# First loads on two queues, products of ones ahead of the first weights, and squares summed by additions

## The chip, the cores and the metric

The kernel runs on one core of a Trainium2 chip. The metric is the device time of one execution in microseconds (us); lower is better. Times below are of single executions, and the median of several is compared.

## The reference

Two transformer blocks run one after the other on one sequence of 256 tokens with 2048 channels. The first ("hybrid") block normalises its input, multiplies by a wide weight matrix, and joins a forgetting attention with a recurrent (RWKV-like) branch. The second normalises again and joins a gated convolution, a latent attention and an attention over 256 memory tokens. What matters here is the root mean square norm, which stands at the head of each block, before the memory attention and inside the latent attention:

```python
def rms_norm(x, g):
    xf = x.astype(jnp.float32)
    y = xf * lax.rsqrt(jnp.mean(xf * xf, axis=-1, keepdims=True) + EPS)
    return (y * g.astype(jnp.float32)).astype(x.dtype)

h = _rmsnorm(x, norm_gain)
u = h @ w_in
```

All arithmetic is float32. The output is 256 x 2048.

## The kernel before

**Data and tiles.** Activations lie channel-major: a tile of kind `a4` holds 4 x 128 channels (128 partitions, 4 slices) of 256 tokens, so four such tiles hold an activation of 2048 channels. Weights come from memory in 658 blocks of 128 x 1024 floats (`raw`). `conv_to` (L399) splits every block into a high part, copied by ScalarE (`whi`, L407), and a rest, subtracted by VectorE (`wlo`, L408). A product with float32 precision is then three products in the faster float32r format (high x high, high x low, low x high). `mm` (L284) records every product, so all of them carry the line L287; `tt` (L240) records two-operand VectorE work at L242, `red` (L268) records reductions at L270, `act` (L272) all ScalarE work at L279.

**The beginning.** `par`, the table of gains, is loaded at L325 by SyncE's queue. `dma_to` (L380) loads in this order, all on the same queue: two halves of the first input tile `xt[0]` (L388), each followed by a half of the first weight block (L389), then whole blocks and the other three input tiles (L392, L396). The kernel does not wait for the norm before it multiplies: `start_tile` (L666) scales a tile by the gain and splits it into `xgh` and `xgl`, products with the groups `lora` and `r0` are accumulated over the four tiles (the loop at L716), and the results are scaled by the reciprocal root at the end. Beside this, `start_squares` (L680) squares each tile on ScalarE (`sq`, 128 x 1024) and sums the four channel slices on VectorE with one reduction over a transposed view (L683, `sqr`, 128 x 256). In the fourth round, four products with a matrix of ones (L724, `ssq`) add up over partitions and tiles, and `mean_rsqrt` (L645) turns the sum into the reciprocal root `rs`.

**The same sum elsewhere.** `sumsq_start` (L632), called by the memory job `mem_job` (L1279), has for each of four tiles a square, a reduction and a product with ones. `latent_job` (L1414), called for `cq` and `ckv`, has one square, one reduction (L1420) and one product with ones.

**The order of the work.** Large products are called group by group (`gemm`, L472). Smaller jobs are generators, spawned into a list; after each piece of a group `pump` (L459) steps them as far as a book of estimated engine times allows (`clock`, L232): each recorded operation adds an estimate to its engine's clock. The framework then arranges the recorded instructions of each engine by a simulated timeline; for example, the memset of L794 stands at 0.89 us and the load of L806 at 6.47 us, far ahead of their places in the code. On the chip every engine runs its list in that fixed order.

Of the kernel before, what the change touches and what calls it, by code (L numbers as in the profile page):

```python
# [14 lines left out]
ALU = mybir.AluOpType  # L15
# [212 lines left out]
def hybrid_kernel(ctx: ExitStack, tc: tile.TileContext, io, out):  # L228
    nc = tc.nc
    TE, ACT, DVE, POOL = nc.tensor, nc.scalar, nc.vector, nc.gpsimd  # L230
# [3 lines left out]
    def fsz(ap):  # L234
        n = 1
        for s in ap.shape[1:]:
            n *= s
        return n
# [5 lines left out]
    def mul(o, a, b):  # L244
        tt(o, a, b, ALU.mult)
# [22 lines left out]
    def red(o, a, op):  # L268
        clock["dve"] += CD + fsz(a) / 960.0
        DVE.tensor_reduce(out=o, in_=a, axis=AX.X, op=op)  # L270

    def act(o, a, f, scale=1.0, bias=None, accum=None):  # L272
        clock["act"] += CA + fsz(o) / 1200.0
        kw = {}
        if bias is not None:
            kw["bias"] = bias
        if accum is not None:
            kw["accum_out"] = accum
        ACT.activation(out=o, in_=a, func=f, scale=scale, **kw)  # L279
# [4 lines left out]
    def mm(o, l, r, start=True, stop=True):  # L284
        n = fsz(o)
        clock["pe"] += max(0.000424 * n, 0.0001 + 0.0016 * fsz(l) / 2) if l.dtype == F32R else max(0.00168 * n, 0.00168 * fsz(l))
        TE.matmul(o, lhsT=l, rhs=r, start=start, stop=stop)  # L287
# [13 lines left out]
    def nm(s):  # L301
        serial[0] += 1
        return f"{s}_{serial[0]}"

    def a4(name, dt=F32):
        return apool.tile([128, 4, 256], dt, name=nm(name), tag="a4")

    def b1(name, dt=F32, shape=(128, 256)):
        return spool.tile(list(shape), dt, name=nm(name), tag="b1")
# [7 lines left out]
    def bank(name):  # L317
        return ppool.tile([128, 512], F32, name=nm(name), tag="s")


    par = cpool.tile([128, NPAR], F32, name="par")
    con = cpool.tile([128, NCON2], F32, name="con")
    con1 = cpool.tile([128, NCON - NCON2], F32, name="con1", tag="early_late2")
    xt = [a4("xt") for _ in range(4)]
    nc.sync.dma_start(out=par, in_=io["params"])  # L325

    def pc(n, i=0, k=1, p0=0, p1=128):
        o = PCOL[n][0]
# [12 lines left out]
    one1 = cpool.tile([128, 1], F32, name="one1")  # L341
    DVE.memset(one1, 1.0)
    ones = one1.to_broadcast([128, 128])

    omm = cpool.tile([128, 34], F32, name="omm")
    hw0 = cpool.tile([128, 8], F32, name="hw0")
# [6 lines left out]
    def derive_params():  # L353
        mu0 = PCOL["mu_r"][0]
        ts(omm, par[:, mu0:mu0 + 34], -1.0, ALU.mult, 1.0, ALU.add)
        ts(hw0, pc("w0", 0, 8), 0.5, ALU.mult)
        ts(ha0, pc("a0", 0, 8), 0.5, ALU.mult)
        ts(ka2, pc("k_a", 0, 8), 0.5, ALU.mult)
        ts(oka, pc("k_a", 0, 8), -0.5, ALU.mult, 1.0, ALU.add)
        ts(qns, par[:, PCOL["qn_g"][0]:PCOL["qn_g"][0] + 2], 192.0 ** -0.5, ALU.mult)  # L360
        ts(mqs, pc("mqn_g", 0, 2), 256.0 ** -0.5, ALU.mult)
# [9 lines left out]
    def block_at(i):  # L371

        if i >= 12:
            return i
        return 4 + 2 * (i // 3) + i % 3 - 1 if i % 3 else i // 3

    def half(p):
        return slice(512 * p, 512 * p + 512)

    def dma_to(n):  # L380
        while st["dma"] < min(n, nblk):
            i = st["dma"]
            j = block_at(i)
            raw_t[j] = wpool.tile([128, 1024], F32, name=nm("raw"), tag="raw", bufs=NRAW)
            x = i // 3
            if i == 0:
                for p in range(2):
                    nc.sync.dma_start(out=xt[0][:, 2 * p:2 * p + 2, :], in_=io["xT"][:, 2 * p:2 * p + 2, :])  # L388
                    nc.sync.dma_start(out=raw_t[j][:, half(p)], in_=io["W"][j, :, half(p)])  # L389
            else:  # L390
                if i % 3 == 0 and x < 4:
                    nc.sync.dma_start(out=xt[x], in_=io["xT"][:, 4 * x:4 * x + 4, :])  # L392
                if i == 12:
                    nc.sync.dma_start(out=lw2f[0:96, :], in_=io["w2"])
                    nc.sync.dma_start(out=la2f[0:96, :], in_=io["a2"])
                nc.sync.dma_start(out=raw_t[j], in_=io["W"][j])  # L396
            st["dma"] += 1
# [155 lines left out]
    def new_pair(name):  # L553
        return a4(name + "h", F32R), a4(name + "l", F32R)
# [7 lines left out]
    def out4(name, dt=F32):  # L562
        return claim(a4(name, dt))
# [23 lines left out]
    def run(gen):  # L587
        for _ in gen:
            pass
# [39 lines left out]
    la2f = la2.rearrange("p a b -> p (a b)")  # L629
    dma_to(NRAW)  # L630

    def sumsq_start(tiles, scales=None):  # L632

        ps = bank("ssq")
        n = len(tiles)
        for i, x in enumerate(tiles):
            sq = a4("sq")
            act(sq, x, AF.Square)
            r = b1("sqr")
            red(r, sq.rearrange("p a t -> p t a"), ALU.add)  # L640
            yield
            mm(ps[:, :256], ones, r, start=i == 0, stop=i == n - 1)
        sumsq_start.out = ps[:, :256]

    def mean_rsqrt(ps, n, eps):  # L645
# [15 lines left out]
            yield  # L661

    xg = []
    r4 = a4("sqr")

    def start_tile(i):  # L666

        x = xt[i]
        p = new_pair("xg")
        xg.append(p)  # L670
        for cs in ((range(2), range(2, 4)) if i == 0 else (range(4),)):
            for c in cs:
                acopy(p[0][:, c, :], x[:, c, :], scale=pc("norm_gain", 4 * i + c))
            for c in cs:
                stt(p[1][:, c, :], x[:, c, :], pc("norm_gain", 4 * i + c), p[0].bitcast(F32)[:, c, :], ALU.mult,
                    ALU.subtract)
            if cs[0] == 0:
                conv_to(3 * i + 1)

    def start_squares(i):  # L680
        sq = a4("sq")
        act(sq, xt[i], AF.Square)
        red(r4[:, i, :], sq.rearrange("p a t -> p t a"), ALU.add)  # L683


    def shifted(dst, ps, key, c, p1=128):
# [23 lines left out]
            shifted(t[:, c, :], xs[:, c, :], key, 4 * b + c)  # L710
        return f

    ssq = bank("ssq")[:, :256]
    acc_l = [bank("lora")[:, :256] for _ in range(2)]
    acc_r = [gpool.tile([128, 512], F32, name=nm("acc.r0"), tag="g")[:, :256] for _ in range(4)]
    for b in range(4):  # L716
        start_tile(b)
        if b == 0:
            derive_params()
        conv_to(3 * b + 3)  # L720
        start_squares(b)
        if b == 3:
            for i in range(4):
                mm(ssq, ones, r4[:, i, :], start=i == 0, stop=i == 3)  # L724
            run(mean_rsqrt(ssq, 2048.0, 1e-6))
            rs = mean_rsqrt.out
            lr, evac = out4("lr"), evac_scaled("r", 0)
            conv_to(14)
        for acc, cols, blocks in ((acc_l, 256, [b]), (acc_r, 512, [4 + 2 * b, 5 + 2 * b])):
            per = 1024 // cols  # L730
            for c, o in enumerate(acc):
                for e, j in enumerate(blocks):
                    for i in range(per):
                        k = per * e + i
                        w = slice(i * cols + 128 * c, i * cols + 128 * c + 128)
                        xh, xl = xg[b][0][:, k, :], xg[b][1][:, k, :]
                        mm(o, hi_t[j][:, w], xh, start=b == 0 and k == 0, stop=False)
                        mm(o, hi_t[j][:, w], xl, start=False, stop=False)
                        mm(o, lo_t[j][:, w], xh, start=False, stop=b == 3 and k == 3)
                if b == 3:  # L740
                    if cols == 256:
                        key = ("wd", "ad")[c]
                        lora[key] = lr[:, 2 + c, :]
                        mul(lr[:, c, :], o, rs)
                        shifted(lora[key], lr[:, c, :], key, 0)
                    else:
                        evac(c, o)
            for j in blocks:
                del hi_t[j], lo_t[j]
    del ssq, r4  # L750

    def start_job():
        yield from norm_pairs(xt, lambda c: pc("norm_gain", c), rs, "h", h)
# [630 lines left out]
    def rope_tables():  # L1384
# [5 lines left out]
        ts(a, a, cc("invf"), ALU.mult)  # L1390
        ts(k, a, 1.0 / (2.0 * math.pi), ALU.mult, MAGIC, ALU.add)
        ts(k, k, -MAGIC, ALU.add)
        yield
# [20 lines left out]
    def latent_job(d, gain, name):  # L1414
        t = d[0]
        ps = bank("lss")
        sq = a4("lsq")
        act(sq, t, AF.Square)
        r = b1("lr")
        red(r, sq.rearrange("p a t -> p t a"), ALU.add)  # L1420
        yield
        mm(ps[:, :256], ones, r)
        yield
        ms = b1("lms")
        ts(ms, ps[:, :256], 1.0 / 512.0, ALU.mult, 1e-6, ALU.add)
        y, tmp, g = b1("ly"), b1("lt"), b1("lg")
        yield from rsqrt(ms, y, tmp, g)
        for c in range(4):
            stt(t[:, c, :], t[:, c, :], pc(gain, c), y, ALU.mult, ALU.mult)
        yield  # L1430
        p = new_pair(name)
        split(t, p[0], p[1])
        lat[name] = [p]
# [260 lines left out]
    for j in range(4):  # L1694
        p = out_pair("ol")
# [10 lines left out]
    for j in range(4):  # L1706
        gemm(f"gl{j}", h2, gate(gt))
        p = out_pair("mg")
# [17 lines left out]
        gemm(f"w2{j}", mg, evac_out(j))  # L1726


MAGIC = 12582912.0
TWO_PI = (6.28125, 0.0019350051879882812, 3.0199159819567e-07)  # L1730
NA4, NB1, NB2 = 33, 7, 5
# [39 lines left out]
```

## Time and profile before

| | before |
|---|---|
| median of 3 runs | 2058.69 us |
| lowest, highest run | 2053.68, 2060.20 us |
| the profiled execution's own time | 2059.04 us |
| its span from the first to the last instruction | 2057.2 us |
| PE busy | 2023.2 us (98%) |
| VectorE (DVE) busy | 1348.6 us (66%) |
| ScalarE (ACT) busy | 968.9 us (47%) |
| mean granted TensorE clock | 0.995 |

PE is TensorE's matrix product, PEld its weight load, SPq the queue that SyncE issues, "L287" line 287 of the kernel. A row of a timeline has the start, the duration of the group (both in us), engine, line, operation, the written tile and the read ones, their shapes, and in brackets how long the engine had been idle and what ended that. The chain of waits is the work that ended last, followed back from the last instruction.

### The profile page before, as it was taken

The numbers are of one execution on the slowest core, as the hardware profiler recorded it, in microseconds if no ns is written. First come the engines' busy times: TensorE is split into PE (matmuls) and PEld (weight loads), VectorE is DVE, ScalarE is ACT, GpSimd is POOL, SyncE is SP. The second block draws the span as 40 slices with busy tenths as digits, with TensorE's granted clock in tenths as the row PEclk, the third lists the DMA queues.
The fourth block names the chain that finished last, engine by engine and source line by source line (L and its number), as shares of the span: only waits on it lengthen the run. The fifth ranks groups of instructions, "written<-read, shape, count | busy, mean of one in ns | idle before, by whom it ended". The sixth has DMA issues, their size and how long they took to land.

```text
span 2057.2 us, 33333 instructions
## 1 busy us (share of the span) xinstructions
PE 2023.2 (98%) x13456; PEld 1820.6 (88%) x13456; DVE 1348.6 (66%) x1987; ACT 968.9 (47%) x1334; POOL 73.9 (4%) x133
## 2 busy tenths in 40 slices
PE   8999989999899999999999999999999999999999
PEld 8999889998677888898999899998788889988887
DVE  8776966879745578665865676755765655555554
ACT  6634435454344445554555445445545444444442
POOL 0002000010000000000000000000000000000000
PEclk9999999999999999999999999999999999999999
DMA  7555543645544756665655554556665655566664
GB/s 248 172 175 165 172 139 128 185 149 169 182 144 141 268 187 215 190 220 185 190 183 183 158 182 154 186 164 195 205 189 170 203 168 182 195 208 202 193 195 153
DMA packets 105674, 374.97 MB, mean 182 GB/s; under 512 B 12920, under 2 KB 13904, under 8 KB 105520
## 3 DMA queue, kind: packets, MB, share of 16 engines
q1 hardware_dynamic: 97568, 350.73, 53.1%
q0 software_dynamic: 7952, 22.12, 3.6%
q8 instruction: 105, 1.72, 0.4%
q14 instruction: 49, 0.40, 0.1%
HBM read 365.76 MB, written 5.86 MB: 181 GB/s over the span
## 4 chain that ended last, share of the span: by engine, by line
PE 89%; DVE 6%; issue 2%; DMA 2%; ACT 1%; POOL 0%; SPq 0%; DVEq 0%; ACTq 0%; POOLq 0%
PE acc.lz L287 4%; PE acc.gb L287 4%; PE acc.gl L287 4%; PE acc.gc L287 4%; PE acc.wo L287 4%; PE acc.w L287 4%; PE acc.lo L287 4%; PE acc.gm L287 4%; DVE wlo L242 2%; PE acc.fq L287 2%; PE acc.mz L287 2%; PE acc.mq L287 2%; PE acc.cz L287 2%; PE acc.cb L287 2%; PE acc.mk L287 2%; PE acc.zb L287 2%
## 5 line engine op out<-in xcount | busy, mean ns | idle before, releaser
L242 DVE TENSOR_TENSOR wlo<-raw,whi 128x1024 fp32r<-128x1024 f32 (+1 forms) x659 | 795.6, 1221 | 493.2 <-ACT whi L279 481.7
L279 ACT ACTIVATE whi<-raw 128x1024 fp32r<-128x1024 f32 (+1 forms) x659 | 683.3, 1055 | 758.6 <-issue 88.0
L287 PE MATMUL acc.lz<-h2h,whi 128*128 128x256 f32 x256 | 72.5, 283 | 0.0
L287 PE MATMUL acc.lz<-h2l,whi 128*128 128x256 f32 x256 | 72.5, 283 | 0.0
L287 PE MATMUL acc.lz<-h2h,wlo 128*128 128x256 f32 x256 | 72.4, 283 | 0.0
L287 PE MATMUL acc.ga<-wlo,hh 128*128 128x512 f32 x128 | 52.3, 410 | 1.9 <-DVE wlo L242 1.9
L287 PE MATMUL acc.gb<-whi,hh 128*128 128x512 f32 x128 | 50.1, 400 | 1.1 <-ACT gate L279 1.1
L287 PE MATMUL acc.ga<-whi,hl 128*128 128x512 f32 x128 | 51.1, 404 | 0.0
L287 PE MATMUL acc.gb<-wlo,hh 128*128 128x512 f32 x128 | 50.6, 399 | 0.0
L287 PE MATMUL acc.gb<-whi,hl 128*128 128x512 f32 x128 | 50.4, 398 | 0.0
L287 PE MATMUL acc.ga<-whi,hh 128*128 128x512 f32 x128 | 50.3, 403 | 0.0
L287 PE MATMUL acc.gl<-wlo,h2h 128*128 128x512 f32 x128 | 50.0, 392 | 0.0
L287 PE MATMUL acc.gl<-whi,h2h 128*128 128x512 f32 x128 | 50.0, 392 | 0.0
L242 DVE TENSOR_TENSOR W<-W,W 64x1 f32<-64x1 f32 (+30 forms) x62 | 48.7, 785 | 2.1
L287 PE MATMUL acc.gc<-whi,h2l 128*128 128x512 f32 x128 | 50.0, 392 | 0.0
L287 PE MATMUL acc.gl<-whi,h2l 128*128 128x512 f32 x128 | 50.0, 392 | 0.0
L287 PE MATMUL acc.w<-wlo,mgh 128*128 128x512 f32 x128 | 49.9, 390 | 0.0
L287 PE MATMUL acc.w<-whi,mgl 128*128 128x512 f32 x128 | 49.9, 390 | 0.0
L287 PE MATMUL acc.gm<-wlo,h2h 128*128 128x512 f32 x128 | 49.9, 391 | 0.0
L287 PE MATMUL acc.gc<-wlo,h2h 128*128 128x512 f32 x128 | 49.9, 391 | 0.0
L287 PE MATMUL acc.gm<-whi,h2l 128*128 128x512 f32 x128 | 49.8, 390 | 0.0
L287 PE MATMUL acc.wo<-whi,ml 128*128 128x512 f32 x128 | 49.5, 389 | 0.0
(627 smaller groups left out, 6223.9 us busy)
## 6 DMA issues: line engine op xcount, KB each, us to landing
raw<-in_W SPq DMA_DIRECT2D x657, 512.0 KB, 4.0
hr<-hd POOLq DMA_DIRECT2D x10, 512.0 KB, 5.2
hr<-hd POOLq DMA_DIRECT2D x12, 256.0 KB, 6.5
xr<-in_xtm POOLq DMA_DIRECT2D x4, 512.0 KB, 6.3
mt<-in_memT POOLq DMA_DIRECT2D x4, 512.0 KB, 6.2
xbd<-x1g POOLq DMA_DIRECT2D x4, 512.0 KB, 3.0
xo<-xbd POOLq DMA_DIRECT2D x4, 512.0 KB, 5.3
out_tm<-xo SPq DMA_DIRECT2D x8, 256.0 KB, 4.5
```

The costliest lines, as they stand in the source:

```text
L242: DVE.tensor_tensor(out=o, in0=a, in1=b, op=op)
L279: ACT.activation(out=o, in_=a, func=f, scale=scale, **kw)
L287: TE.matmul(o, lhsT=l, rhs=r, start=start, stop=stop)
```

## The change

Three things are changed.

1. The loads of `par` and of the two halves of `xt[0]` are issued by ScalarE's queue instead of SyncE's. The halves of the first weight block and everything after them stay on SyncE's.
2. Right after the ones are set, five products of ones with ones (128 x 128 by 128 x 256, float32) are written into the `ssq` bank, which is allocated there instead of ahead of the loop. Their results are overwritten later by the first use.
3. The reduction over the four slices becomes additions (`fold`): the two upper slices are added to the two lower ones in place (128 x 512), then the two remaining slices go into a running sum `r` (128 x 256; one addition for the first tile, two for each further one). The four products with ones, at the beginning and in `sumsq_start`, become one product of the running sum. `latent_job` uses `fold` in place of its reduction and keeps its one product.

```diff
-    nc.sync.dma_start(out=par, in_=io["params"])
+    nc.scalar.dma_start(out=par, in_=io["params"])
...
     ones = one1.to_broadcast([128, 128])
+    ssq = bank("ssq")[:, :256]
+    for _ in range(NWARM):
+        TE.matmul(ssq, lhsT=ones, rhs=one1.to_broadcast([128, 256]), start=True, stop=True)
...
-                    nc.sync.dma_start(out=xt[0][:, 2 * p:2 * p + 2, :], in_=io["xT"][:, 2 * p:2 * p + 2, :])
+                    nc.scalar.dma_start(out=xt[0][:, 2 * p:2 * p + 2, :], in_=io["xT"][:, 2 * p:2 * p + 2, :])
                     nc.sync.dma_start(out=raw_t[j][:, half(p)], in_=io["W"][j, :, half(p)])
...
-    def sumsq_start(tiles, scales=None):
+    def fold(sq, r, i):
+
+        add(sq[:, 0:2, :], sq[:, 0:2, :], sq[:, 2:4, :])
+        if i:
+            add(r, r, sq[:, 0, :])
+            add(r, r, sq[:, 1, :])
+        else:
+            add(r, sq[:, 0, :], sq[:, 1, :])
+
+    def sumsq_start(tiles):
 
         ps = bank("ssq")
-        n = len(tiles)
+        r = b1("sqr")
         for i, x in enumerate(tiles):
             sq = a4("sq")
             act(sq, x, AF.Square)
-            r = b1("sqr")
-            red(r, sq.rearrange("p a t -> p t a"), ALU.add)
-            yield
-            mm(ps[:, :256], ones, r, start=i == 0, stop=i == n - 1)
+            fold(sq, r, i)
+            yield
+        mm(ps[:, :256], ones, r)
         sumsq_start.out = ps[:, :256]
...
-    r4 = a4("sqr")
+    r0 = b1("sqr")
...
-        red(r4[:, i, :], sq.rearrange("p a t -> p t a"), ALU.add)
+        fold(sq, r0, i)
...
-            for i in range(4):
-                mm(ssq, ones, r4[:, i, :], start=i == 0, stop=i == 3)
+            mm(ssq, ones, r0)
...
         r = b1("lr")
-        red(r, sq.rearrange("p a t -> p t a"), ALU.add)
+        fold(sq, r, 0)
...
+NWARM = 5
```

More of the change, by code (lines that the diff above doesn't have):

```diff
@@ L711, in evac_scaled @@
         return f
-    ssq = bank("ssq")[:, :256]
     acc_l = [bank("lora")[:, :256] for _ in range(2)]
@@ L749, in hybrid_kernel @@
                 del hi_t[j], lo_t[j]
-    del ssq, r4
+    del ssq, r0
     def start_job():
```

## The prediction

> **What bounds the kernel now.** I read the page's first part, then its chain of waits.
>
> ```profile
> PE 2023.2 (98%) x13456; PEld 1820.6 (88%) x13456; DVE 1348.6 (66%) x1987; ACT 968.9 (47%) x1334; POOL 73.9 (4%) x133
> PE 89%; DVE 6%; issue 2%; DMA 2%; ACT 1%; POOL 0%; SPq 0%; DVEq 0%; ACTq 0%; POOLq 0%
> ```
>
> TensorE is busy for 2023.2 of 2057.2 us and holds 89% of the chain. Outside the stretches where something else ends last, only an edit that takes work from PE shortens the time. The change sits mostly in the first 30 us, so I took the chain and the timeline of each engine there.
>
> ```profile
> 0.74 0.38 SPq L325 DMA_DIRECT2D par<-in_params  x1
> 1.18 0.42 SPq L388 DMA_DIRECT2D xt<-in_xT  x1
> 1.65 0.42 SPq L389 DMA_DIRECT2D raw<-in_W  x1
> 0.73 1.28 ACT L279 ACT_TABLE_LOAD   x1 [0.73 <-PEq L1763]
> 5.57 0.63 ACT L279 ACTIVATE whi<-raw 128x512 fp32r<-128x512 f32 x1 [3.55 <-DMA raw<-in_W]
> 6.10 0.89 ACT L279 ACTIVATE xgh<-xt,par 128x256 fp32r<-128x256 f32 x2
> 6.65 0.79 PE L287 MATMUL lora<-xgh,whi 128*128 128x256 f32 x2 [6.65 <-ACT xgh L279]
> 22.29 1.24 DVE wlo L242
> 23.57 5.06 PE acc.r L287 x40
> ```
>
> The first half block is issued third, at 1.65, and lands just before 5.57, when ScalarE can start; the first product follows at 6.65. The last two lines are from the chain in order of time: up to 23.57 the start goes through loads and VectorE, there PE waits for a `wlo`, and from then on the chain is PE's. So the start is worth what moves VectorE's work ahead of 23.57; what PE saves before that is only slack.
>
> **The change part by part.**
>
> *Loads on two queues.* The half block moves from third to first in SyncE's queue, from 1.65 to 0.74: 0.91 us. ScalarE has nothing to do until 5.57, so its three issues (0.38 and twice 0.42) cost it nothing, and behind them on its list stands only that first copy. If `par` and the halves of `xt` stay ahead of the table load, they leave at 0.74, 1.18 and 1.65, each no later than before. If the table load stays first, they begin at 2.01, 1.27 us later than now, and `xgh` at 6.10 has an unknown slack against that. Bounds: 0.91 gained to 1.3 lost. Bytes do not change, so I take 0.7, near the first end, because ScalarE waits there for the weight block and not for `xt`. Every later load on SyncE's queue (blocks, then the other input tiles) stands three issues, 0.38 + 0.42 + 0.43 = 1.2 us, further ahead; while these share the DMA engines with ScalarE's three they can delay each other, which is inside the bounds.
>
> ```profile
> 3.00:4.00 1.00, 0.00 (x0) 0.00 (x0) 0.40 (x6) 0.00 (x0) 0.00 (x0) 1.00 0.96 291
> 5.00:6.00 1.00, 0.00 (x0) 0.00 (x0) 0.00 (x0) 0.43 (x1) 0.00 (x0) 1.00 0.58 166
> ```
>
> The table by windows (last columns: share of the 16 DMA engines, GB/s) shows the engines at 0.96 from 3 to 4 us, and at 0.58 from 5 to 6. The Trainium skill's DMA: Bandwidth & Descriptors, Issuing engines are not separate DMA queues, says that loads issued by several engines run on the same 16 engines and that only the issue time is saved. By that rule this part is at most the 0.91 above; the 0.96 agrees, while the dip to 0.58 would leave room for more if the rule were wrong, up to 0.42 of that microsecond.
>
> *Squares by additions.* The reductions and the rows nearest to the additions:
>
> ```profile
> 9.33 1.96 DVE L270 TENSOR_REDUCE sqr<-sq 128x256 f32<-128x1024 f32 x1 [0.46 <-ACT sq L279]
> 11.21 2.95 DVE L242 TENSOR_TENSOR wlo<-raw,whi 128x512 fp32r<-128x512 f32 x3
> 15.66 2.06 DVE L270 TENSOR_REDUCE sqr<-sq 128x256 f32<-128x1024 f32 x1
> 17.63 1.22 DVE L242 TENSOR_TENSOR wlo<-raw,whi 128x1024 fp32r<-128x1024 f32 x1
> 20.34 2.04 DVE L270 TENSOR_REDUCE sqr<-sq 128x256 f32<-128x1024 f32 x1
> 22.29 2.37 DVE L242 TENSOR_TENSOR wlo<-raw,whi 128x1024 fp32r<-128x1024 f32 x2
> L242 DVE TENSOR_TENSOR mf<-mf,pr 128x512 f32<-128x512 f32 x8 | 5.5, 683 | 0.0
> L242 DVE TENSOR_TENSOR ht<-ht,hms 128x256 f32<-128x256 f32 x32 | 13.5, 422 | 0.6
> 36.81 0.42 DVE L242 TENSOR_TENSOR t<-rsn 128x256 f32<-128x256 f32 x1
> 37.27 0.42 DVE L242 TENSOR_TENSOR t<-t,ms 128x256 f32<-128x256 f32 x1
> ```
>
> From its start to the next start a reduction holds VectorE for 1.88, 1.97 and 1.95 us. An addition of 128x512 takes 0.68, one of 128x256 0.42; a dependent one starts 0.04 after its forerunner's end (36.81 to 37.27), while unrelated ones overlap by 0.07 (a `wlo` takes 1.22, the pair at 22.29 takes 2.37). So the first fold is 0.68 + 0.04 + 0.42 - 0.07 = 1.07, a later one 0.68 + 0.04 + 0.42 + 0.04 + 0.42 - 0.07 = 1.53. Saved ahead of the `wlo` at 22.29: 0.81 + 0.44 + 0.42 = 1.7 us. Bounds: 1.1 if each of the eight additions costs 0.07 more, 2.2 if the five dependent ones overlap too. VectorE runs without a gap from 11.21, so this is on the path. The page VectorE: DVE Perf Modes of the Trainium skill (The perf-mode tier table) puts reductions at 1x speed; by its formula for 1x work, (N+151)/0.96 ns, 1024 elements would be an estimated 1.22 us, the three folds would lose 0.7 instead of saving 1.7, and the whole sum below would be 1.3 instead of 3.7. The rows disagree (1.96 to 2.06 us), so it gets no chance.
>
> Together VectorE's work ahead of 23.57 comes 0.7 + 1.7 = 2.4 us earlier.
>
> *Products of ones.* PE in the same stretch:
>
> ```profile
> 8.18 0.41 PE L287 MATMUL lora<-xgl,whi 128*128 128x256 f32 x1
> 8.39 0.41 PE L287 MATMUL lora<-xgh,wlo 128*128 128x256 f32 x1
> 6.00:12.00 6.00, 5.06 (x20) 4.25 (x20) 5.04 (x8) 5.18 (x9) 0.00 (x0) 1.00 0.97 374
> 206.87 20.18 PE acc.fk L287 x168
> L287 PE MATMUL ssq<-sqr,one x16: 377/378/482, 11.3 to 788.4; 128*128 128x256 f32 x16
> 780.84 0.43 PE ssq L287 x2
> 788.31 0.43 PE ssq L287 x2
> ```
>
> Starts are 0.21 apart at 8.18, and later the same size takes 20.18 / 168 = 0.12: of the 20 products that begin before 12 us some 17 run at about half pace, 17 x 0.09 = 1.5 us. The eight float32 products with ones are 16 instructions, pairs of 0.43 at full pace. Five products of ones are ten such instructions; at half pace a pair costs 0.86, so 4.3 us from 0.9 (after the memset) to 5.2, ahead of a first product at 6.65 - 0.7 = 5.95. They cost nothing while that gap of 0.75 holds; without it, the overrun. If they lift the pace, PE alone could be 0.7 + 1.5 + 3 x 0.43 (three `ssq` products gone) = 3.5 ahead at 23.57. It still waits for `wlo`, which is 2.4 ahead. So their worth here is 0, and at most 3.5 - 2.4 = 1.1 if the framework's order lets PE go past that `wlo`. If they fail to lift the pace, PE is 2.0 ahead and the start is worth 2.0 instead of 2.4.
>
> *One product instead of four.* At the start this is in the 3.5. In the memory job three pairs fall away where PE has no gap:
>
> ```profile
> 780.00:800.00 20.00, 20.00 (x93) 16.63 (x92) 15.27 (x26) 8.74 (x12) 2.15 (x4) 1.00 0.75 257
> 726.90 2.04 DVE L270 TENSOR_REDUCE sqr<-sq 128x256 f32<-128x1024 f32 x1
> ```
>
> PE is busy 20.00 of 20.00 us, so 3 x 0.43 = 1.3 us is won whole. The one product now waits for the last fold; the last reduction ended at 728.9, 59 us before the last product, so no wait replaces it; at the start the last of the four already waited for the fourth sum. VectorE's lighter sums in the memory job and the two latent jobs save nothing, being hidden by PE, and cost nothing if that cover goes.
>
> **The sum.** 2.4 + 1.3 = 3.7 us. The profiled execution took 2059.04, 0.35 above the median of 2058.69; so 2055.3 for it and 2055.0 for a median. Own range by the bounds: the loads losing 1.3 and the folds saving 1.1 leave only the 1.3 of the memory job, 2057.4; PE at its own limit, 3.5 + 1.3, gives 2053.9.
>
> **The rivals.** What moves more than these terms is where PE stands idle later:
>
> ```profile
> PE u L287 <- DMA XA<-Xd: 5.8, 3, 3.3
> 280.00:290.00 10.00, 8.14 (x165) 7.60 (x165) 2.46 (x3) 3.29 (x4) 1.09 (x2) 0.83 0.88 222
> 540.00:550.00 10.00, 9.21 (x39) 6.70 (x37) 9.81 (x9) 3.18 (x3) 0.55 (x1) 1.00 0.52 173
> 550.00:560.00 10.00, 6.60 (x25) 5.13 (x26) 5.89 (x6) 2.13 (x2) 4.46 (x7) 0.85 0.97 279
> 560.00:570.00 10.00, 10.00 (x87) 7.83 (x87) 2.16 (x2) 3.30 (x4) 0.00 (x0) 0.64 0.41 88
> 640.00:650.00 10.00, 8.73 (x22) 6.25 (x23) 4.14 (x6) 6.76 (x11) 0.00 (x0) 0.66 0.06 16
> 227.48 1.24 DVE wlo L242
> 578.21 5.66 PE acc.pf L287 x24
> ```
>
> The granted clock (the column before the DMA share) falls after each gap: as it is 1.0 or one half, the means stand for 3.4, 3.0 + 7.2 and 6.8 us at half, 20.4 in all, worth up to 10.2 us of PE. The Trainium skill's TensorE: Matmul & The Clock Gate (Part 1) says that the gate watches a free-running window of about 3.4 us; the 3.4, 10.2 and 6.8 agree, being one, three and two of them. A start shifted by a few us meets these windows at another place, and so may every execution: the three runs already differ by 6.5.
>
> *Faster than forecast.* Half of the dips go away with the shift: 10.2 / 2 = 5.1 more, 2050. For it: their lengths hang on gaps of 1 to 3 us. Against it: the gaps themselves, waits for the DMA behind VectorE's recurrence, are not touched. Chance 0.22.
>
> *Gain swallowed.* From 540 to 550 VectorE is busy 9.81 of 10: if its recurrence does not move with PE, PE arrives 2.4 earlier and waits 2.4 longer for `XA`; only the memory job's 1.3 stays: 2057.4. Against it: the chain enters such a stretch from PE (`acc.fk` from 206.87, then the `wlo` at 227.48), whose progress sets when weights are split. Chance 0.15.
>
> *Slower.* The order is dealt anew. The planner's book loses 3 x 0.43 of PE at the start, and its estimate of each later fold (1.26 against 1.13) and first fold (0.93) differs too, so `pump` may step the recurrence one piece of a group apart from now. If `u` thereby stands 24 products earlier in PE's list (5.66 us by the row at 578.21) at both places, PE idles 11 us more: 2055 + 11 = 2066. It decides where `XA` lands later than PE's list asks. Against it: the book is clamped at every step, so 1.3 us is soon forgotten. Chance 0.08.
>
> **How the numbers follow.** Forecast 0.55, swallowed 0.15, faster 0.22, slower 0.08. About 0.3% (6.2 us; the runs' own spread is 6.5) is what a measurement here can tell from no change. Forecast and swallowed lie within it: 0.70; 0.22 beyond 2052.5, 0.08 beyond 2064.9. The range from 2049 to 2061 takes the forecast, the swallowed case and most of the faster one, and leaves the slower and the faster one's far end.
>
> **What would show it.** Right: first `whi` at about 4.9 and first product near 5.9; folds of about 1.07 and 1.53 us; product starts 0.12 apart from the first; the chain turning to PE near 21.2; two `ssq` instructions instead of eight by 790. Wrong: a first product later than 6.65 (the loads), a chain that is PE's from 6 us on (PE was the bound), `u` waiting much more than 5.8 us or a changed sum of low clock (the order and the dips outweigh the edit).

## The result and the profile after

The changed kernel took 2067.35 us (median of 22 runs, 2060.93 to 2076.75), the kernel before on the same chip 2058.20 (22 runs, 2053.51 to 2062.64): a ratio of 1.0050, 95% interval 1.0041 to 1.0059. This ratio and those below are worked out from the single runs and are not the quotients of the medians beside them (here 1.0044). The change makes the kernel slower by 0.5%, and the forecast was 2055.0 in a range of 2049 to 2061: wrong in sign and outside the range. The profiled execution of after took 2065.81 us with a span of 2064.0. Two executions at a much lower clock (2457.36 us in run 10, 2102.24 us in before beside runs 5 to 8) are left out of the ratios, and one whose clock is on record as 0.946 at an ordinary 2061.27 us is left out of the splits by clock below.

The first part of the page of after, and the shares of its chain:

```profile
PE 2028.1 (98%) x13454; PEld 1823.6 (88%) x13454; DVE 1342.5 (65%) x2003; ACT 969.6 (47%) x1334; POOL 74.0 (4%) x133
PE 85%; DVE 7%; DMA 4%; issue 2%; ACT 1%; POOL 0%; SPq 0%; DVEq 0%; ACTq 0%; POOLq 0%
```

TensorE does nearly the same work, but holds 85% of the chain instead of 89%. The list of TensorE's waits names the place (us in total, times, longest):

```profile
PE acc.kr L287 <- ACT hh L279: 6.2, 1, 6.2
PE u L287 <- DMA XA<-Xd: 5.3, 2, 3.2
```

The first line is new, and nothing like it stands in the list of before, while the wait of `u` that the slower rival looked at is no longer than it was (5.8). `acc.kr` is the first group of products that needs the normalised tile `hh`. The chain of after in order of time leads back from it:

```profile
21.17 5.06 PE acc.r L287 x40
...
34.87 0.43 PE ssq L287 x2
35.30 2.87 PE lora L287 x24
38.17 4.93 PE acc.r L287 x41
...
45.36 0.75 DVE lr L242 x2
46.11 1.32 DVE xs L242 x4
47.43 1.59 DVE nf L262 x4
49.02 0.02 issue
49.04 1.06 ACT hh L279
50.10 0.04 issue
50.15 1.22 PE acc.kr L287 x4
```

The same in before, one row from the chain and two from the timelines of ScalarE and TensorE:

```profile
29.11 0.43 PE ssq L287 x2
```

```profile
41.56 1.04 ACT L279 ACTIVATE hh<-nf 128x1024 fp32r<-128x1024 f32 x1
46.27 0.40 PE L287 MATMUL acc.kr<-hh,whi 128*128 128x256 f32 x2
```

In before the last product of the sum of squares ran at 29.11, `hh` was done 13.5 us later, at 42.60, and TensorE came to `acc.kr` only at 46.27: 3.7 us of slack. In after the only product ran at 34.87, and `acc.kr` followed 15.28 us later, as soon as `hh` was there. The start itself had gained what was forecast: 50.15 - 6.2 = 43.95 is when TensorE was ready for `acc.kr`, 2.3 ahead of 46.27. Then it lost 6.2.

VectorE shows that the sum was not late, only its product. First after, then before:

```profile
27.66 0.41 DVE L242 TENSOR_TENSOR sqr<-sqr,sq 128x256 f32<-128x256 f32 x1
31.08 1.23 DVE L242 TENSOR_TENSOR wlo<-raw,whi 128x1024 fp32r<-128x1024 f32 x1 [0.74 <-ACT whi L279]
35.16 1.22 DVE L242 TENSOR_TENSOR wlo<-raw,whi 128x1024 fp32r<-128x1024 f32 x1 [2.85 <-ACT whi L279]
36.31 0.41 DVE L258 TENSOR_SCALAR ms<-ssq 128x256 f32<-128x256 f32 x1
43.27 0.42 DVE L242 TENSOR_TENSOR rsn<-rsn,t 128x256 f32<-128x256 f32 x1
44.22 1.23 DVE L242 TENSOR_TENSOR wlo<-raw,whi 128x1024 fp32r<-128x1024 f32 x1 [0.53 <-ACT whi L279]
47.35 1.66 DVE L262 SCALAR_TENSOR_TENSOR nf<-xt,par,rsn 128x256 f32<-128x256 f32 x4
```

```profile
31.50 0.42 DVE L258 TENSOR_SCALAR ms<-ssq 128x256 f32<-128x256 f32 x1
38.05 0.42 DVE L242 TENSOR_TENSOR rsn<-rsn,t 128x256 f32<-128x256 f32 x1
39.53 1.67 DVE L262 SCALAR_TENSOR_TENSOR nf<-xt,par,rsn 128x256 f32<-128x256 f32 x4
```

The folds of after were finished at 28.07. TensorE took up the sum 6.8 us later, having run other products in between; VectorE meanwhile stood idle for 0.74 and 2.85 us. From the product to `hh` VectorE has an order of its own: `ms` waits behind one `wlo`, the steps of the reciprocal root are interleaved with more, and a `wlo`, `lr` and `xs` now stand ahead of `nf`, where before only a `wlo` did. That `wlo` at 44.22 waits in turn for a `whi` of ScalarE, and this one for the end of `acc.r`:

```profile
43.12 2.00 ACT L279 ACTIVATE whi<-raw 128x1024 fp32r<-128x1024 f32 x2 [3.98 <-PE acc.r L287]
```

So in the chain of after the step from TensorE to VectorE is this `whi`, and not the reciprocal root, which was ready at 43.69 (43.27 + 0.42). `nf` started 3.66 us after that; in before it started 1.06 us after the root (38.47 to 39.53).

In the gap the clock falls, and it is still low when the work goes on. The table by windows of after (the column after POOL's is the granted clock):

```profile
47.00:50.00 3.00, 0.00 (x0) 0.00 (x0) 3.00 (x7) 2.27 (x5) 0.00 (x0) 0.51 0.32 128
50.00:55.00 5.00, 4.85 (x17) 4.18 (x17) 5.00 (x12) 1.02 (x3) 0.00 (x0) 0.61 0.49 178
```

The reason stands in the compiled program: the order of the lists, TensorE's first. The framework arranges each engine's instructions by a simulation of its own. In before the last of the four `ssq` products is number 152 of TensorE's products and the first `acc.kr` number 293: 140 products lie between. In after the one product is number 218 and `acc.kr` 291: 72 lie between, 72 x 0.12 = 8.6 us. The way through VectorE and ScalarE takes 15.28 from the start of the product, 0.43 of it the product itself; 15.28 - 0.43 - 8.6 = 6.2, which is the wait. The length of this way hangs on VectorE's order too. By the rows above, an estimate: 3.66 - 1.06 = 2.6 of the 6.2 us pass because `lr` and `xs`, and a `wlo` that waits, stand between the root and `nf`, and the other 3.6 because the product is late. Both orders come out of the same simulation; no run changed VectorE's order alone.

### The profile page after: what moved, and what is told of

Read it like the earlier page. It is cut to its first block, busy times and chain, and to the rows that moved or that the text cites. A ratio compares the mean times of both kernels' runs of the same rounds, so it can differ in the third digit from the quotient of the medians.

```text
span 2064.0 us, 33343 instructions
## 1 busy us (share of the span) xinstructions
PE 2028.1 (98%) x13454; PEld 1823.6 (88%) x13454; DVE 1342.5 (65%) x2003; ACT 969.6 (47%) x1334; POOL 74.0 (4%) x133
## 4 chain that ended last, share of the span: by engine, by line
PE 85%; DVE 7%; DMA 4%; issue 2%; ACT 1%; POOL 0%; SPq 0%; DVEq 0%; ACTq 0%; POOLq 0%
PE acc.lz L287 4%; PE acc.gl L287 4%; PE acc.w L287 4%; PE acc.wo L287 4%; PE acc.lo L287 4%; PE acc.gc L287 4%; PE acc.gb L287 4%; PE acc.gm L287 4%; DVE wlo L242 3%; PE acc.fq L287 2%; PE acc.vr L287 2%; PE acc.mz L287 2%; PE acc.mq L287 2%; PE acc.cz L287 2%; PE acc.mk L287 2%
## 5 line engine op out<-in xcount | busy, mean ns | idle before, releaser
L287 PE MATMUL acc.w<-whi,mgh 128*128 128x512 f32 x128 | 49.4, 390 | 0.0
```

## The experiments

Theory: the loss is the place of that product (with what the framework arranges behind it), the wait that follows, and the clock that falls behind the wait. Rivals: the second load queue, the products of ones or the additions cost time themselves. Each group of runs is timed against the kernel before on the same chip, whose median was 2056.14, 2056.52, 2056.48 and 2056.64 us for the four groups (1 to 4, 5 to 8, 9 to 11, 12 to 15). "Between" counts TensorE's products between the last `ssq` product and the first `acc.kr`.

| run | between | wait at `acc.kr`, us | median us | ratio (95%) |
|---|---|---|---|---|
| before | 140 | none | | 1 |
| after | 72 | 6.2 | 2067.35 | 1.0050 (1.0041 to 1.0059) |
| 1 loads alone | 72 | 6.2 | 2065.09 | 1.0049 (1.0032 to 1.0066) |
| 2 loads, products of ones | 140 | none | 2060.49 | 1.0022 (1.0009 to 1.0036) |
| 3 additions alone | 72 | 6.2 | 2066.74 | 1.0053 (1.0034 to 1.0072) |
| 4 before, last product late | 72 | 6.2 | 2065.84 | 1.0053 (1.0034 to 1.0072) |
| 5 after, four products | 120 | 2.3 | 2057.90 | 1.0005 (0.9991 to 1.0020) |
| 6 after, product at high priority | 106 | 2.7 | 2060.98 | 1.0025 (1.0012 to 1.0038) |
| 7 after, filler products | 72 and 12 fillers | 1.0 | 2061.02 | 1.0014 (1.0000 to 1.0028) |
| 8 additions in memory and latent jobs only | 140 | none | 2055.42 | 1.0002 (0.9990 to 1.0015) |
| 9 five products of ones alone | 140 | none | 2064.11 | 1.0036 (1.0022 to 1.0050) |
| 10 after, reductions kept at the start | 140 | none | 2062.17 | 1.0019 (1.0002 to 1.0037) |
| 11 four products, fourth tile hoisted | 122 | 2.3 | 2059.26 | 1.0008 (0.9992 to 1.0023) |
| 12 after without products of ones | 72 | 6.2 | 2067.22 | 1.0059 (1.0047 to 1.0071) |
| 13 one product of ones alone | 140 | none | 2057.94 | 1.0008 (0.9994 to 1.0021) |
| 14 eight products of ones alone | 140 | none | 2062.65 | 1.0029 (1.0018 to 1.0039) |
| 15 run 11 without products of ones | 138 | none | 2056.64 | 1.0001 (0.9992 to 1.0010) |

**1. Loads alone.** Before, with the three loads moved to ScalarE's queue.

```diff
-    nc.sync.dma_start(out=par, ...)
+    nc.scalar.dma_start(out=par, ...)
-    nc.sync.dma_start(out=xt[0][...], ...)
+    nc.scalar.dma_start(out=xt[0][...], ...)
```

> The kernel before with part 1 alone (first loads on ScalarE's queue). In TensorE's fixed list the last of the four products of the sum then stands at row 219 instead of 152, the first product that needs the normalised tile at 292 instead of 293. Place theory (the late place of that product delays the reciprocal root, TensorE idles before acc.kr and its clock drops): 2064 to 2069 us, a wait of 5 to 8 us before the first acc.kr, although nothing is folded. Addition theory (the folds load VectorE's list): 2056 to 2059. Queue theory (loads on two queues disturb each other): 2062 to 2069, and the next run as slow.

Measured 1.0049, with the wait of 6.2 us. The chain in order of time:

```profile
22.38 1.14 DVE wlo L242
23.52 0.04 issue
23.57 5.05 PE acc.r L287 x40
...
37.55 0.43 PE ssq L287 x2
```

That is in the range of the place theory. Two things follow. The loads alone gain nothing at the start: the chain turns to PE at 23.57, as before. And they make the whole loss, though no product or addition was changed: the last of the four `ssq` products went from number 152 to 219.

**2. Loads and products of ones.** The edit of run 1, and

```diff
+    ssq = bank("ssq")[:, :256]
+    for _ in range(NWARM):
+        TE.matmul(ssq, lhsT=ones, rhs=one1.to_broadcast([128, 256]), start=True, stop=True)
```

> Parts 1 and 2 (loads on ScalarE's queue, five products of ones), no folds. The last product of the sum stands at row 153. Place theory: 2055 to 2059 us, no wait over 1 us before the first acc.kr. Queue theory: 2062 to 2069. Warm-up theory (products of ones spoil the start or the clock): 2062 to 2069. Addition theory: 2055 to 2059.

The place is early again (number 153), the wait is gone, and so is over half of run 1's loss. The median, 2060.49, lies above what the theory expected (2055 to 2059), and no row at the start shows why. Runs 9, 13 and 14 take this up.

**3. Additions alone.** Before with `fold` in all three places and one product instead of four; loads as before, no products of ones.

```diff
-            red(r, sq.rearrange("p a t -> p t a"), ALU.add)
+            fold(sq, r, i)
...
-            for i in range(4):
-                mm(ssq, ones, r4[:, i, :], start=i == 0, stop=i == 3)
+            mm(ssq, ones, r0)
```

> Part 3 alone (additions, one product, everywhere). The one product of the first sum stands at row 217. Place theory: 2063 to 2068 us, a wait of 5 to 8 us before the first acc.kr, 1.3 us won back in the memory job. Addition theory: 2063 to 2069 as well. Queue and warm-up theories: 2055 to 2058.

The one product stands at number 217: the wait of 6.2 us, 1.0053. So two edits with nothing in common lose the same, and together (after, run 12) they lose no more. Costs of their own would add up.

**4. The place by itself.** Before, with nothing changed but the order: the last of the four products is held, by a dependency that only orders TensorE's list, behind the last product of the third tile. For that, `conv_to(14)` is written ahead of the last product; the diff is shortened.

```diff
-            for i in range(4):
-                mm(ssq, ones, r4[:, i, :], start=i == 0, stop=i == 3)
+            for i in range(3):
+                mm(ssq, ones, r4[:, i, :], start=i == 0, stop=False)
...
+            last = mm(ssq, ones, r4[:, 3, :], start=False, stop=True)
+            tc.add_manual_dep(last.ins, done[0].ins.name, ...)
```

> The kernel before, with none of the three parts, but the last of the four products of the first sum is bound behind the last product of the third tile, which puts it at row 220 of TensorE's list instead of 152. Same work, same loads, same reductions. Place theory: 2064 to 2069 us, with the wait before the first acc.kr and the clock drop after it. All other theories: 2056 to 2060.

Its list of waits and its chain:

```profile
PE acc.kr L287 <- ACT hh L279: 6.2, 1, 6.2
```

```profile
36.69 0.43 PE ssq L287 x2
...
51.98 1.22 PE acc.kr L287 x4
```

Loads, reductions and all four products are those of before, and the time is 1.0053. 36.69 to 51.98 is 15.29, against 15.28 in after. The late place makes the whole loss with none of the three parts in the kernel: this settles it against the rivals. It does not separate the place from VectorE's order, since the framework deals that anew as well: in this chain `lr` (47.18), `xs` (47.93) and `nf` (49.26) follow each other as in after.

**5. Four products again.** After, but each tile keeps its sum, and four products follow, as in before. The lists change again: number 173, 120 between.

```diff
-        fold(sq, r0, i)
+        fold(sq, r4[:, i, :], 0)
-            mm(ssq, ones, r0)
+            for i in range(4):
+                mm(ssq, ones, r4[:, i, :], start=i == 0, stop=i == 3)
```

> The changed kernel with folds, but at the start each tile keeps its own sum and four products of ones, as before; the memory job keeps its one product. The last product of the first sum stands at row 173, with 120 products up to the first acc.kr at row 294. Place theory: the way from that product to the first acc.kr took 15.3 us in all four runs with a late place, and 120 products take 14.4 us, so the wait there is 0.5 us (0 to 1.5) and the clock does not drop after it; 2 us slower to 3 us faster than the kernel before. Addition theory: as slow as the changed kernel, 7 to 11 us over the kernel before, since all additions are there.

1.0005: the loss is gone, with loads, products of ones and additions all in. The wait is 2.3, more than expected, because `hh` stands on ScalarE behind a `whi`. On VectorE `lr` and half of `xs` stand ahead of `nf` here too. This gap, too, is followed by a lower clock:

```profile
46.00:56.00 10.00, 8.30 (x45) 7.48 (x46) 10.00 (x20) 6.52 (x10) 0.00 (x0) 0.83 0.47 144
```

**6. The product at high priority.** After, with the one product written under the framework's high priority. It moves from 218 to 184.

```diff
-            mm(ssq, ones, r0)
+            with tc.high_priority():
+                mm(ssq, ones, r0)
```

> The changed kernel, only that the one product of the first sum is recorded with high priority; it comes to row 184, with 106 products up to the first acc.kr. Place theory: 15.3 - 0.4 - 12.7 = 2.1 us of wait (1 to 3.5), no clock drop or one window; 0 to 5 us slower than the kernel before. Addition theory: 7 to 11 us slower.

A wait of 2.7 us and 1.0025, half the loss, at the upper end of the 0 to 5 us expected. Runs 5, 6 and 11 stand with 120, 106 and 122 products between, and with 1.0005, 1.0025 and 1.0008; at 72 the ratio is 1.0049 to 1.0059.

**7. The gap filled.** After, with 12 products of ones that nobody reads put behind the last product of the start, so that PE is busy in the gap.

```diff
     del ssq, r0
+    wm = bank("wm")[:, :256]
+    for _ in range(12):
+        TE.matmul(wm, lhsT=ones, rhs=one1.to_broadcast([128, 256]), start=True, stop=True)
```

> The changed kernel with 12 more products of ones between the last acc.r and the first acc.kr, so that TensorE works while it would wait. They take 12 x 0.43 = 5.2 us of the wait of 6.2. If the clock drop after the wait is part of the loss, lz and acc.kr run at full pace and 2 to 3.5 us of the changed kernel's loss come back: 5 to 8 us slower than the kernel before. If the wait alone counts: 8 to 10 us slower.

```profile
50.29 0.75 PE L287 MATMUL acc.kr<-hh,whi 128*128 128x256 f32 x4 [1.01 <-ACT hh L279]
```

```profile
46.00:56.00 10.00, 8.85 (x50) 7.40 (x49) 9.97 (x23) 5.02 (x10) 0.00 (x0) 1.00 0.32 107
```

`acc.kr` starts as late as in after (50.29 against 50.15), but the clock stays at 1.00, and the ratio falls from 1.0050 to 1.0014, a loss of 2.9 us (0 to 5.8) where 5 to 8 were expected. The difference is some 7 us. The profiles explain little of it: in after the clock was at half for 6.8 us, but for 3.0 of them TensorE stood idle; the 3.9 us of work at half pace lose 1.9, and by the chains the two kernels are 1.2 us apart behind the low clock (the next products of `acc.kr` at 55.28 in after, 54.04 here). So the low clock is part of the loss at this place; what the rest of the gain is isn't shown.

**8. Additions in the memory job and the latent jobs only.** Before, with the start left alone.

```diff
-            red(r, sq.rearrange("p a t -> p t a"), ALU.add)
+            fold(sq, r, i)
...
-            mm(ps[:, :256], ones, r, start=i == 0, stop=i == n - 1)
+        mm(ps[:, :256], ones, r)
```

> The kernel before with the folds and the one product in the memory job and the two latent jobs alone; the start is untouched, the last product of the first sum stands at row 152. Place theory and my sum: 1.3 us faster (three pairs of 0.43), between 3 us faster and 1 us slower. If the folds or the waiting single product harm the memory job: 1 to 5 us slower.

1.0002: no change can be told, and nothing of the harm that the rival expected. The chain shows where the three products went; the last of four ended at 788.74 in before, and here the one product stands at

```profile
787.22 0.43 PE ssq L287 x2
```

Counted over the job, `acc.wo` halfway is reached 1.32 us earlier against before than the start of that job was, which is the 1.3 of the prediction; it is too small for the median to show.

**9. Five products of ones alone.** Before, with the edit shown in run 2 (`NWARM = 5`) and nothing else.

```diff
+    for _ in range(NWARM):
+        TE.matmul(ssq, lhsT=ones, rhs=one1.to_broadcast([128, 256]), start=True, stop=True)
```

> Before, with the five products of ones at the start alone; the loads, the reductions, the four products and their places in TensorE's list stay as they are (the last of the four sums' products 141 rows ahead of the first acc.kr). Theory (the loss is the sum's product moved to a late place): 2055 to 2058 us, within 0.2% of before, no wait above 1 us ahead of the first acc.kr. Rival (the loads or the products of ones cost 0.2% by themselves, as the run with both showed 1.0022): 2059 to 2062 if it is the products of ones, and then no row near the start would show it.

The theory's expectation failed: 2064.11, 1.0036, without a wait at `acc.kr`, and more than the rival's 2059 to 2062 as well. At the start PE shows

```profile
0.93 3.99 PE L346 MATMUL ssq<-one 128*128 128x256 f32 x10 [0.93 <-DVE one L342]
7.17 0.51 PE L287 MATMUL lora<-xgh,whi 128*128 128x256 f32 x2 [2.25 <-ACT xgh L279]
```

and the profiled execution is level with before up to 147 us: `acc.kr` starts 0.1 us earlier than in before. So if they cost time, this execution does not show it there.

**10. Reductions kept.** After, with reductions and four products at the start; loads, products of ones and the later additions stay.

```diff
-        fold(sq, r0, i)
+        red(r4[:, i, :], sq.rearrange("p a t -> p t a"), ALU.add)
-            mm(ssq, ones, r0)
+            for i in range(4):
+                mm(ssq, ones, r4[:, i, :], start=i == 0, stop=i == 3)
```

> After, with the reductions and the four products kept at the start; loads on two queues, products of ones, and the additions with one product in the memory job and the latent job stay. The last of the four products stands 141 rows ahead of the first acc.kr, as in before. Theory: the wait of 6.2 us there is gone (0 to 0.5), the start is level with before, the memory job keeps its 1.3 us: 2054 to 2058 us. Rival (loads and products of ones cost about 0.2%): 2058 to 2062.

The wait of 6.2 is gone, and of the loss 0.3% of 0.5%. The theory's 2054 to 2058 failed; the median, 2062.17, is at the upper bound of what the rival expected; the interval (1.0002 to 1.0037) reaches from nothing to most of run 2's and run 9's.

**11. The fourth tile hoisted.** Run 5, with the fourth tile's copy, squares, additions and products written ahead of the third round's products.

```diff
...
+            if b == 2 and cols == 256:
+                start_tile(3)
+                start_squares(3)
+                for i in range(4):
+                    mm(ssq, ones, r4[:, i, :], start=i == 0, stop=i == 3)
+                run(mean_rsqrt(ssq, 2048.0, 1e-6))
```

> After, with four sums and four products at the start, and the fourth tile's copy, squares, additions and products written ahead of the third round's products, which puts the last of the four at row 171 of TensorE's list (one product alone, as in after: 218). Theory: a wait of 1 to 2.5 us ahead of the first acc.kr at most, 2055 to 2060 us. Rival (the additions themselves, and not the place, cost the time): 2063 to 2067.

As the theory expected: a wait of 2.3 us, 2059.26, 1.0008 (0.9992 to 1.0023). No cost of the additions by themselves can be told. Unlike in run 5, no low clock follows this gap.

**12. After without products of ones.**

```diff
-    for _ in range(NWARM):
-        TE.matmul(ssq, lhsT=ones, rhs=one1.to_broadcast([128, 256]), start=True, stop=True)
```

> After without its products of ones (the sum's one product stays late: row 217 of TensorE's list, first acc.kr at 290). Theory (place alone): the wait of 6.2 us and the low clock behind it are all there: 2064 to 2068 us, as after. Rival (the products of ones cost a further 0.2 to 0.36% wherever they stand, as the two runs with them and the early place showed): 2058 to 2062, so that the place would be worth only part of the loss.

1.0059, the wait of 6.2 us is all there. Whatever the products of ones do in runs 2 and 9, they are no part of the loss of the change: with them it loses 0.50%, without them 0.59%, and the intervals overlap.

**13 and 14. One and eight products of ones.** Run 9 with `NWARM` at 1 and at 8.

```diff
-NWARM = 5
+NWARM = 1
```

> Before with one product of ones instead of the five of the run before that took 1.0036; the lists are the same but for that. If the five cost time by raising the clock early and dropping it again at 8 us: 2055 to 2058 (one product of 0.9 us doesn't raise the clock before 10 us). If they cost time by being there at all (their bank taken earlier, another build): 2061 to 2066, as with five.

> Before with eight products of ones instead of five, which fill the 2.3 us between the last of the five and the first product of the first weights. If the five cost time by the clock that drops at 8 us after that gap: no drop there, 2053 to 2057. If by being there at all: 2061 to 2066. If by being late themselves: a wait on them ahead of the first product, at most 1 us.

One took 1.0008, where no cost can be told, eight 1.0029. So it isn't the mere presence of such a product. The second idea is that five end too early, so that the clock that they raised falls again at about 8 us, as it does in run 9. It fails too: with eight, which leave a gap of 0.3 us ahead of the first product, the clock does not fall there, nor does it in run 2, and both are slower all the same. Five or eight such products cost the kernel some 0.3%, and by which wait stays open. The place is not the start, as far as one execution of each can tell: in that of run 14 TensorE is within 1 us of before up to 558 us and 5.9 behind at 1459, in stages that the edit does not touch.

**15. The early place, without products of ones.** Run 11 without its products of ones: number 152, 138 between.

```diff
-    for _ in range(NWARM):
-        TE.matmul(ssq, lhsT=ones, rhs=one1.to_broadcast([128, 256]), start=True, stop=True)
```

> Loads on two queues and all additions, no products of ones, four sums with four products at the start, and the fourth tile's copy, squares, additions and products written ahead of the third round's products: the last of the four stands at row 152, the first acc.kr at 291, 139 apart as in before. Theory (place): no wait above 1 us there, the memory job's 1.3 us kept: 2053 to 2057. Rival (additions or loads cost time by themselves): 2060 or more.

2056.64, 1.0001 (0.9992 to 1.0010): no wait at `acc.kr`, all loads moved, all additions in. In the profiled execution PE is 1.3 us ahead of before at `acc.kr` and 4.1 ahead in the middle of the memory job, yet the median is that of before. No version beat the kernel before.

## Why the prediction was wrong

**The step that failed** is "so no wait replaces it", with its reason for the start, "the last of the four already waited for the fourth sum". It took the one product to stay where the last of the four had been. The sum it waits for was in fact ready (28.07 after, 28.20 before), but in after the product did not run when its data were there; it ran at 34.87, when its turn in TensorE's list came. The compiled list put it 66 products later, the way from it to `acc.kr` is 15.3 us long, and 8.6 us of products were left to cover it: a wait of 6.2 us that the sum had put at nothing. Run 4 shows that this late place, with the order of VectorE that comes with it, makes the whole loss.

**The slower rival** had the right kind, an order dealt anew, and the wrong place: it looked at the planner's book and at `u` before `XA`, and gave it 0.08. The wait of `u` did not grow. A test that the prediction did not make stood closer: which instruction at the head of a long chain might be moved, and how much slack that chain has. In the trace of before it had 3.7 us, about 31 products of 0.12, and the change moved its head by 66 places.

**The size.** The clock and the span of every run split the loss. The 22 runs of after have a mean span of 2065.6 us at a mean clock of 0.9931; 34 runs of before beside runs 5 to 8 have 2054.9 at 0.9959. Span times clock is the time at full pace: 2051.3 against 2046.5, 4.9 more. The remaining 14.3 against 8.4, 5.8 more, goes to the low clock. Runs 3 and 4 split likewise: 5.9 and 5.7 at full pace, 4.6 each by the clock, against 18 runs of before. Runs 1 and 12, with the same wait, split as 4.4 and 5.0, and as 3.4 and 8.0. In these five, 44 to 70% of the loss stands as low clock; but that part holds the time at half that fell into the gap itself and dips in later stages too, so it is not the price of this gap alone. In the profile of after, TensorE was 2.3 us ahead of before when the wait began and 5.2 behind at the middle product of `acc.kr` (124.2 us in before): 7.6 us for a wait of 6.2. The prediction had the fall of the clock after gaps of 1 to 3 us in its rows, and used it only for dips that might go away.

**Loads on two queues.** In the timelines of SyncE, ScalarE and TensorE of after:

```profile
0.74 0.86 SPq L392 DMA_DIRECT2D raw<-in_W  x2
0.73 0.41 ACTq L325 DMA_DIRECT2D par<-in_params  x1
1.17 0.94 ACTq L391 DMA_DIRECT2D xt<-in_xT  x2
3.83 0.63 ACT L279 ACTIVATE whi<-raw 128x512 fp32r<-128x512 f32 x1 [0.41 <-DMA raw<-in_W]
5.38 0.63 ACT L279 ACTIVATE whi<-raw 128x512 fp32r<-128x512 f32 x1 [0.92 <-DMA raw<-in_W]
6.46 0.50 PE L287 MATMUL lora<-xgh,whi 128*128 128x256 f32 x2 [0.90 <-ACT xgh L279]
```

The queue did as forecast: the block leaves first, at 0.74, and `par` and `xt` at 0.73 and 1.17, ahead of the table load. The first `whi` came even earlier than said (3.83, not 4.9). But the second half's `whi` now stands ahead of `xgh`, and the first product starts at 6.46, 0.2 ahead of 6.65 and not 0.7. Alone the loads were worth 0 where the chain turns to PE (run 1). The term was too large, and the moved gain stopped at the next copy.

**Folds.** In VectorE's timeline of after:

```profile
15.31 0.68 DVE L242 TENSOR_TENSOR sq<-sq 128x512 f32<-128x512 f32 x1
17.05 0.41 DVE L242 TENSOR_TENSOR sqr<-sqr,sq 128x256 f32<-128x256 f32 x1
18.96 0.42 DVE L242 TENSOR_TENSOR sqr<-sqr,sq 128x256 f32<-128x256 f32 x1
```

0.68, 0.41 and 0.42, as in the sum, though other work stands between them. The chain turned to PE at 21.17 where 21.2 was forecast, 2.4 earlier than in before. That the total was right is luck: the loads alone gave 0 of their 0.7 (run 1), and the additions alone (run 3), priced at 1.7, brought TensorE 2.2 us ahead at 28.5 us.

**Products of ones.** They ran from 0.92 for 4.63 us, to 5.55 instead of 5.2, in time for the first product. They did lift the pace: from 7.41 on product starts are 0.12 apart, where before had 0.21.

```profile
7.41 0.28 PE L287 MATMUL lora<-xgh,wlo 128*128 128x256 f32 x1
7.52 0.28 PE L287 MATMUL lora<-xgh,whi 128*128 128x256 f32 x1
```

The clock column can't tell this, as it reads 1.00 from 6 to 12 us in before too. Priced at nothing, which holds inside the change (run 12 against after), not for five or eight of them in the kernel before (runs 9 and 14). How the same edit costs 0.3% there and nothing here is open.

**One product in the memory job.** Two instructions instead of eight, as foretold:

```profile
L287 PE MATMUL ssq<-sqr,one x4: 377/378/378, 34.7 to 796.2; 128*128 128x256 f32 x4
```

Four in all (two per sum) instead of 16, and 1.32 us earlier in the profile of run 8.

**Swallowed.** Even where the loss was gone the 3.7 us did not come: runs 5, 8, 11 and 15 lie between 1.0001 and 1.0008, and run 15's interval leaves at most 0.0008 x 2056.6 = 1.6 us of gain. The rival that most of it is swallowed is the one that these runs favour, though not shown by the mechanism that it named. Split by clock as above, run 15 needs 1.6 us less than before at full pace and loses 1.9 more to the low clock, run 11 1.3 less and 3.5 more. These differences have standard errors of 0.6 to 1.2 us, so they point to the clock and do not prove it.

## What to carry to other kernels

Where a framework orders the instructions, an edit also deals the order: before pricing one, look for the instruction at the head of each long side chain, count the work that covers it in the list of the bounding engine, and compare that with the length of the chain, whose own steps may be dealt anew as well. In the kernel before the two were 17.2 (29.11 to 46.27) and 13.5 us, so the place of one product of 0.43 us could be worth more than all terms of the sum. After the edit, compare the lists first, and fill or shorten a gap of TensorE with the clock in mind.

## What the hardware showed that was not expected

A gap of 6.2 us cost TensorE 7.6 to 9.5 us by the start of the middle product of `acc.kr` (after and runs 1, 3, 4, 12). Half pace set in inside the gap, 2.2 to 4.2 us after its beginning, and lasted 6.8 us (after, runs 3 and 12) or 10.2 us (runs 1 and 4), 3.9 to 7.8 of it on work. Smaller gaps did so too: after 2.3 us in run 5 the windows show 3.4 us of half pace, and after 2.7 us in run 6 6.8 us:

```profile
46.00:56.00 10.00, 9.74 (x43) 8.58 (x44) 9.89 (x20) 6.11 (x10) 0.00 (x0) 0.66 0.40 143
```

The Trainium skill's TensorE: Matmul & The Clock Gate (Why this matters for your kernels) advises no idle gaps of over about 3 us between bursts. Here gaps of 2.3 and 2.7 us were followed by half pace as well, and the measurement decides; but another of 2.3 us (run 11) was not, nor was one of 1.0 us (run 7). So a gap's length alone did not settle it. Twelve products that nobody reads, 24 instructions of 0.21 us in the gap, held the clock, and the kernel with them lost 0.14% instead of 0.50%; in the profile 1.2 us of that stand at this place.
